# Four groups of TensorE transposes in a two-layer trunk handed to transposing transfers, with the attention's list of work rewritten

## The chip, the cores and the metric

The kernel runs on one core of one Trainium2 chip. The metric is the device time of one execution in microseconds (us). Before the change three runs gave 966.21 us in the median (965.93 to 966.33). One more execution was recorded by the hardware profiler; all rows below come from that one.

## The reference, cut to what matters

Two layers, 256 tokens, width 1024, fp32. Each layer is a feed-forward block, a mixer and another feed-forward block. The mixer of layer 0 is a gated recurrence, that of layer 1 is attention with a forget gate:

```python
# layer 0, mixer
gx = x @ w_in                                  # (256, 2 * 1344)
gate, rec = gx[..., :D_RNN], gx[..., D_RNN:]
rec = causal_depthwise_conv(rec, conv_w, conv_b)
rec = rg_lru(rec, w_a, b_a, w_x, b_x, lam)     # a scan over the tokens
return (jax.nn.gelu(gate) * rec) @ w_out
# layer 1, mixer, for each block of 128 tokens
logits = q @ k.T + c_q - c_k                   # 16 heads of 64, masked
p = jax.nn.softmax(logits, axis=-1)
o = p @ v
return o @ w_o
```

`jax.nn.gelu(gate)` comes out of its matrix product with tokens on the partitions, while the scan runs with channels on the partitions, so the gate has to be turned before the two are multiplied. The probabilities `p` likewise have to be turned before the product with `v`.

## The kernel before, in words

The 256 tokens are two halves, t=0 and t=1, of 128. Every large product is made of three fp32r products, high by high, high by low and low by high parts. A weight comes from HBM over SyncE's queue (SP) into one of five buffers `raw`. ScalarE (ACT) copies it to `whi` (L173) and VectorE (DVE) subtracts to get `wlo` (L177). TensorE (PE) then uses the pair for both halves, at L428, L429 and L432 in the feed-forward blocks and the q projection, and at L183 to L192 elsewhere.

PE's order is that of the program text. The work is a list of `items`, each with a preparation (load and split of a weight) and the products for one half. `slot` or `half` runs one of them. `defer(n, fn)` puts a small function n ticks behind, and `queue` with its costs lets out the recurrence's vector work in small portions. The other engines' order is made by a scheduler, which `high_priority` and `keep_in_program_order` steer. DMAs issued by SP stand in SP's order too.

**The recurrence.** `RG_ORDER` lists the items: `0g0` to `0g10` and `1g0` to `1g10` are the gate's products of the two halves, `r` those of the recurrent part, `gw` the small products of the two gates in the scan (L779, with a tanh at L793). A gate item that ends a column group copies its result from PSUM to `tok` (L686) and puts it on the list `plain`, whose Gelu comes later in `roots` (L840); only group 0 of half 0 gets its Gelu at once (L684). After the scan, `batch(g)` calls `gate_T` for both halves: four PE transposes each (L858) into PSUM, from which `product` (L867) multiplies into the scan's result. ACT (L868) and DVE (L873) split that for the output product.

**The attention.** `ATT_ORDER` is a string in which `0` and `1` are the next projection item of a half (first eight of q, then eight of the output), and `l0`, `n0`, `t0`, `v0` are steps of half 0: logits (L1146, sixteen matmuls for two head groups, then bias, row maximum and exponential on DVE and ACT at L1155 to L1162), norm (L1168, L1169), turn (four PE transposes at L1175 and a copy by ACT at L1177), and values (L1189). `l1` and so on are the same of half 1. Half 0 has four head groups of four heads, half 1 eight of two heads.

The q of half 1 is turned by a transfer already: `heads_T` scales it into `htok` (DVE, L996). `planes` (POOL, L212) sorts the fp32 words into two planes of 16-bit halves, `swap` (SP, L216) sends these through a transposing DMA, and `join` (POOL, L220) writes the words into `qT`, for which the logits `l1` wait.

Of the kernel before, what the change touches and what calls it, by code (L numbers as in the profile page):

```python
# [9 lines left out]
F32 = mybir.dt.float32  # L10
# [7 lines left out]
P = 128  # L18
# [25 lines left out]
def trunk_kernel(ctx: ExitStack, tc: tile.TileContext, A: dict, out: bass.AP):  # L44
# [13 lines left out]
    def nm(s):  # L58
        uid[0] += 1
        return f"{s}_{uid[0]}"  # L60
# [7 lines left out]
    def trbank():  # L68
        return psum.tile([P, 512], F32, tag="tr", name=nm("tr"), bufs=2)
# [11 lines left out]
    def defer(n, fn):  # L81
        pend.append([n, fn])
# [127 lines left out]
    def planes(dst, src):  # L210

        nc.gpsimd.tensor_copy(dst.rearrange("p (h f) -> p h f", h=2), src.bitcast(U16).rearrange("p (f h) -> p h f", h=2))  # L212

    def swap(turned, halves):

        tc.keep_in_program_order(nc.sync.dma_start(turned.rearrange("p (a b) -> p a b", b=P), halves, transpose=True))  # L216

    def join(dst, turned):

        nc.gpsimd.tensor_copy(dst, turned.rearrange("p (h f) -> p h f", h=2))  # L220
# [444 lines left out]
    def add_gate_unit(g, k0, kn):  # L665
        c0, nn = GCOLS[g]

        def prep():
            return split(load_raw(w_in(c0, nn, k0, kn), P, kn * nn), P, kn * nn)

        def work(t, u):
            if k0 == 0:
                gacc[(g, t)] = mmbank()
            ps = gacc[(g, t)][:, :nn]
            for j in range(kn):
                k = k0 + j
                mm3(ps, *main_x(t, k), u.hi[:, j * nn:(j + 1) * nn], u.lo[:, j * nn:(j + 1) * nn], k == 0, k == 7)
            if k0 + kn == 8:

                if t not in toks:  # L680
                    toks[t] = pools["r"].tile([P, DRNN], F32, name=f"tok{t}")
                tok = toks[t][:, c0:c0 + nn]
                if (g, t) == (0, 0):
                    nc.scalar.activation(tok, ps, AF.Gelu_apprx_tanh)  # L684
                else:
                    nc.scalar.activation(tok, ps, AF.Copy)  # L686
                    plain.append(tok)
        rg[f"g{sum(n[0] == 'g' and n[1] != 'w' for n in rg)}"] = len(items)
        items.append((prep, work))

    def tiles_of(p):
        return [2 * p, 2 * p + 1] if p < 5 else [10]
# [136 lines left out]
    def batch(g):  # L829

        pairs = [p for p in (2 * g, 2 * g + 1)]
        tps, ys = {}, {}

        def roots():
            for (a, b, w) in parts_of(g):
                v = tt[g][:w, a:b, :]
                nc.scalar.activation(v, v, AF.Sqrt)
            while plain:
                v = plain.pop(0)
                tc.keep_in_program_order(nc.scalar.activation(v, v, AF.Gelu_apprx_tanh))  # L840

        def u_of(p):
            w, m = pw(p), len(tiles_of(p))
            v = tt[g][:w, 2 * (p % 2):2 * (p % 2) + m, :]
            nc.vector.scalar_tensor_tensor(v, th[p][1][:w, :m, :], -1.0, v, ALU.mult, ALU.mult)
            nc.vector.tensor_tensor(v, v, xcs[p][:w, :m, :], ALU.mult)

        def scan(p, j):
            w = pw(p)
            v = tt[g][:w, 2 * (p % 2) + j, :]  # L850
            nc.vector.tensor_tensor_scan(v, th[p][0][:w, j, :], v, 0.0, ALU.mult, ALU.add)

        def gate_T(t):
            tok = toks[t][:, 4 * g * RT:]
            tp = tps[t] = trbank()
            for j in range(len(pairs) * 2 if g < 2 else 3):
                w = width(4 * g + j)
                nc.tensor.transpose(tp[:w, j * P:(j + 1) * P], tok[:, j * RT:j * RT + w], ident)  # L858

        def product(t):  # L860
            y = ys[t] = pools["r"].tile([RT, 4, P], F32, tag="y", name=nm("y"), bufs=2)
            if t == 0:
                yy[g] = [rw.tile([P, 1024], F32R, tag="gy", name=nm("y"), bufs=6).rearrange("p (t a b) -> p t a b", t=2, a=4)
                         for _ in range(2)]
            for (a, b, w) in parts_of(g):
                tp = tps[t][:w, a * P:b * P].rearrange("p (a b) -> p a b", a=b - a)
                nc.vector.tensor_tensor(y[:w, a:b, :], tp, tt[g][:w, a:b, t * P:(t + 1) * P], ALU.mult)  # L867
                nc.scalar.activation(yy[g][0][:w, t, a:b, :], y[:w, a:b, :], AF.Copy)  # L868

        def low(t):  # L870
            yh, yl = yy[g]
            for (a, b, w) in parts_of(g):
                nc.vector.tensor_tensor(yl[:w, t, a:b, :], ys[t][:w, a:b, :], yh[:w, t, a:b, :].bitcast(F32), ALU.subtract)  # L873

        key = ("y", g)
        q = [(0.0, key, roots)]
        for p in pairs:
            s = len(tiles_of(p)) / 2
            q.append((1.3 * s, key, lambda p=p: u_of(p)))
            q += [(0.72, key, lambda p=p, j=j: scan(p, j)) for j in range(len(tiles_of(p)))]  # L880
        q.append((0.0, key, lambda: (gate_T(0), gate_T(1))))
        for t in range(2):
# [26 lines left out]
    def load_gb(key, src):  # L909
        def f():  # L910
            gbox[key] = gain_bcast(src)
        return f
# [211 lines left out]
    def attention(t):  # L1124
# [41 lines left out]
        def norm(hg):  # L1166
            pe, sm = box["pe", hg], box["s", hg]
            nc.vector.reciprocal(sm, sm)  # L1168
            nc.vector.tensor_tensor(pe, pe, sm.unsqueeze(2).to_broadcast([P, per, nk * P]), ALU.mult)  # L1169

        def turn(hg):
            tp = trbank()
            pev = box["pe", hg].rearrange("p a b -> p (a b)")
            for j in range(4):
                nc.tensor.transpose(tp[:, j * P:(j + 1) * P], pev[:, j * P:(j + 1) * P], ident)  # L1175
            pT = box["pT", hg] = ap.tile([P, 4, P], F32, tag="pT", name=nm("pT"), bufs=4)
            nc.scalar.activation(pT.rearrange("p a b -> p (a b)"), tp, AF.Copy)  # L1177
# [25 lines left out]
    for n in range(2):  # L1203
# [2 lines left out]
    row_items(A["attn_w_o"][0], [P] * 8, lambda t, k: (att["oh"][t][:, k, :], att["ol"][t][:, k, :]),  # L1206
              lambda t, accs: enter(t, [main_dest(GI[("ffn2", 1)], t)], accs, gbox["mix1"], False, wait=4),
              rows0=1, late=True)
    ahead(n_q[0] + 2, load_gb("mix1", A["mix_post_g"][1]))
    n_att = len(items)  # L1210


    ffn_items(lambda: pools["f"], A["ffn2_w_gate"][1], A["ffn2_w_up"][1], A["ffn2_w_down"][1], A["ffn2_post_g"][1],
              lambda t: None, last=True)

    ATT_ORDER = ("0 0 0 0 0 0 0 l0 0 1 n0 l0 1 1 t0 n0 1 l0 v0 1 t0 n0 l0 1 v0 n0 1 t0 l1 1 v0 t0 n1 l1 0 v0 "
                 "n1 l1 t1 0 n1 l1 t1 0 n1 l1 v1 v1 t1 0 n1 l1 t1 0 n1 l1 v1 v1 t1 0 n1 l1 t1 0 n1 v1 v1 0 t1 1 "
                 "t1 v1 1 v1 1 1 1 1 1 1")

# [182 lines left out]
    steps = [attention(0), attention(1)]  # L1402
    nxt = [n_ffn3, n_ffn3]
    for c in ATT_ORDER.split():
        if c[0] in "lntv":
            with tc.high_priority():
                steps[int(c[1])][c[0]].pop(0)()
        else:
            half(int(c), nxt[int(c)])
            nxt[int(c)] += 1  # L1410
# [40 lines left out]
```

## Time and profile before

| | |
|---|---|
| median of three runs | 966.21 us |
| profiled execution | 966.79 us, of which 965.1 us are the span |
| PE busy | 957.0 us, 99% of the span |
| DVE, ACT, POOL busy | 639.8, 528.2, 209.1 us |
| PE in the chain that ended last | 95% |
| stage of the recurrence, gate products to turned gates | about 196 to 284 us |
| stage of the attention, half 0 and the q of half 1 | about 720 to 745 us |

A row of the timeline begins with its start and its length in microseconds, then engine, line, operation, what is written and what is read. A bracket at the end gives how long the engine sat idle before it and who released it. Matmuls overlap in the pipeline, so the pace of PE is read from starts, not from lengths.

### The profile page before, as it was taken

How to read it: one execution, taken by the hardware profiler on the slowest of the kernel's cores; microseconds unless marked ns; L12 is line 12 of the kernel's file. 1: busy time of each engine (PE TensorE's matmuls, PEld its weight loads, DVE VectorE, ACT ScalarE, POOL GpSimd, SP SyncE). 2: the span in 40 equal slices, each digit the busy share in tenths (PEclk: the TensorE clock that was granted, in tenths of full speed). 3: DMA queues.
4: the chain of work that ended last, by engine and by line, in shares of the span. 5: the costliest groups of instructions: out<-in, count | busy, mean ns of one | idle time of the engine just before them, and what ended most of it. 6: DMA issues, size and time to landing. Idle time of an engine off the chain costs nothing.

```text
span 965.1 us, 12873 instructions
## 1 busy us (share of the span) xinstructions
PE 957.0 (99%) x4583; PEld 792.3 (82%) x4583; DVE 639.8 (66%) x845; ACT 528.2 (55%) x751; POOL 209.1 (22%) x215
## 2 busy tenths in 40 slices
PE   9999999999999999999999999999999999999997
PEld 6888888898888888888898888888887788888886
DVE  6658764668998666664686566665488876666642
ACT  7446543568886555443565445444366855444431
POOL 2712330100001323230003623224122012232200
PEclk9999999999999999999999999999999999999999
DMA  8788996565337787786558979779763467777731
GB/s 284 227 247 235 267 275 196 156 197 158 121 107 235 204 234 216 202 239 200 136 175 284 248 223 264 225 184 283 237 246 108 133 199 236 207 217 239 221 110 44
DMA packets 146822, 198.27 MB, mean 205 GB/s; under 512 B 65054, under 2 KB 83846, under 8 KB 146630
## 3 DMA queue, kind: packets, MB, share of 16 engines
q1 hardware_dynamic: 144070, 190.53, 66.5%
q0 software_dynamic: 2080, 6.38, 2.3%
q8 instruction: 36, 0.59, 0.3%
q10 hardware_dynamic: 608, 0.53, 0.2%
q14 instruction: 28, 0.23, 0.1%
HBM read 182.19 MB, written 3.16 MB: 192 GB/s over the span
## 4 chain that ended last, share of the span: by engine, by line
PE 95%; DVE 2%; ACT 1%; issue 1%; POOL 0%; DMA 0%; POOLq 0%; DVEq 0%; ACTq 0%
PE mm L428 16%; PE mm L429 16%; PE mm L432 16%; PE mm L183 13%; PE mm L185 13%; PE mm L184 13%; PE gt L779 2%; PE mm L1286 1%; PE mm L190 1%; PE mm L191 1%; PE mm L192 1%; PE gt L226 1%; ACT pe L1162 1%; DVE wlo L177 0%; PE tr L127 0%
## 5 line engine op out<-in xcount | busy, mean ns | idle before, releaser
L177 DVE TENSOR_TENSOR wlo<-raw,whi 128x1024 fp32r<-128x1024 f32 (+5 forms) x329 | 416.5, 1272 | 228.7 <-ACT whi L173 227.7
L173 ACT ACTIVATE whi<-raw 128x1024 fp32r<-128x1024 f32 (+5 forms) x329 | 341.7, 1045 | 305.6 <-PE mm L432 133.5
L428 PE MATMUL mm<-whi,xhi 128*128 128x512 f32 x656 | 256.6, 391 | 0.0
L429 PE MATMUL mm<-wlo,xhi 128*128 128x512 f32 x656 | 255.5, 389 | 0.0
L432 PE MATMUL mm<-whi,xlo 128*128 128x512 f32 x656 | 202.2, 389 | 0.0
L432 PEld LDWEIGHTS mm<-whi,xlo 128*128 128x128 f32 x656 | 123.1, 188 | 26.0 <-DVE xlo L240 0.2
L428 PEld LDWEIGHTS mm<-whi,xhi 128*128 128x128 f32 x656 | 123.2, 188 | 25.8 <-issue 0.7
L429 PEld LDWEIGHTS mm<-wlo,xhi 128*128 128x128 f32 x656 | 123.2, 188 | 25.3 <-DVE wlo L177 0.3
L183 PE MATMUL mm<-whi,hhi 128*128 128x512 f32 x352 | 137.3, 390 | 0.0
L185 PE MATMUL mm<-whi,hlo 128*128 128x512 f32 x352 | 137.0, 389 | 0.0
L184 PE MATMUL mm<-wlo,hhi 128*128 128x512 f32 x352 | 137.0, 389 | 0.0
L540 POOL COPY pl<-prod 128x1024 uint16<-128x1024 uint16 (+1 forms) x48 | 68.4, 1424 | 169.0 <-DMA prod<-pl 168.9
L527 POOL COPY pl<-prod 128x1024 uint16<-128x1024 uint16 (+1 forms) x48 | 65.4, 1362 | 160.4 <-DVE prod L524 91.9
L185 PEld LDWEIGHTS mm<-whi,hlo 128*128 128x128 f32 x352 | 66.1, 188 | 13.8
L184 PEld LDWEIGHTS mm<-wlo,hhi 128*128 128x128 f32 x352 | 66.1, 188 | 13.7
L183 PEld LDWEIGHTS mm<-whi,hhi 128*128 128x128 f32 x352 | 66.1, 188 | 13.7 <-DVE prod L524 0.2
L198 POOL TENSOR_SCALAR nv<-ss 128x1 f32<-128x1 f32 x22 | 9.7, 439 | 284.2 <-ACT junk L205 284.2
L524 DVE SCALAR_TENSOR_TENSOR prod<-mm,rstd,sil 128x512 f32<-128x512 f32 (+1 forms) x48 | 33.8, 703 | 30.7 <-PE mm L432 24.9
L515 ACT ACTIVATE sil<-mm,rstd 128x512 f32<-128x512 f32 (+1 forms) x48 | 31.1, 651 | 33.1 <-PE mm L432 25.2
L546 DVE TENSOR_TENSOR hlo<-pl,hhi 128x512 fp32r<-128x512 f32 (+1 forms) x48 | 40.8, 849 | 5.9 <-ACT hhi L545 5.9
L183 PE MATMUL mm<-whi,xhi 128*128 128x512 f32 (+1 forms) x112 | 42.8, 382 | 0.0
L185 PE MATMUL mm<-whi,xlo 128*128 128x512 f32 (+1 forms) x112 | 42.5, 379 | 0.0
(219 smaller groups left out, 1050.2 us busy)
## 6 DMA issues: line engine op xcount, KB each, us to landing
raw<-in_ffn_w_down_dram SPq DMA_DIRECT2D x88, 512.0 KB
raw<-in_ffn_w_up_dram SPq DMA_DIRECT2D x80, 512.0 KB
raw<-in_ffn_w_gate_dram SPq DMA_DIRECT2D x78, 512.0 KB
raw<-in_rg_w_in_dram SPq DMA_DIRECT2D x10, 504.0 KB
raw<-in_rg_w_out_dram SPq DMA_DIRECT2D x10, 504.0 KB
raw<-in_ffn_w_gate_dram SPq DMA_DIRECT2D x19, 256.0 KB
raw<-in_ffn_w_up_dram SPq DMA_DIRECT2D x16, 256.0 KB
raw<-in_rg_w_in_dram SPq DMA_DIRECT2D x8, 512.0 KB
```

Of the source, the lines that this page charges most:

```text
L173: up = nc.scalar.activation(hi[:parts, c:c + m], rawv[:, c:c + m], AF.Copy)
L177: nc.vector.tensor_tensor(lo[:parts, c:c + m], rawv[:, c:c + m], hi[:parts, c:c + m].bitcast(F32), ALU.subtract)
L183: nc.tensor.matmul(ps, xh, wh, start=first, stop=False)
L184: nc.tensor.matmul(ps, xh, wl, start=False, stop=False)
L185: nc.tensor.matmul(ps, xl, wh, start=False, stop=last)
L428: nc.tensor.matmul(ps, get_x(t, k)[0], u.hi[:, c], start=k == 0, stop=False)
L429: nc.tensor.matmul(ps, get_x(t, k)[0], u.lo[:, c], start=False, stop=False)
L432: nc.tensor.matmul(ps, get_x(t, k)[1], u.hi[:, c], start=False, stop=k == nk - 1)
L524: nc.vector.scalar_tensor_tensor(pr[:, :nn], ps, rs[t][:, 0:1], s, ALU.mult, ALU.mult)
L527: nc.gpsimd.tensor_copy(halves.rearrange("p (h f) -> p h f", h=2), pr[:, :nn].bitcast(U16).rearrange("p (f h) -> p h f", h=2))
L540: nc.gpsimd.tensor_copy(halves.rearrange("p (f h) -> p h f", h=2), turned.rearrange("p (h a) b -> p h (a b)", h=2))
L546: keep(nc.vector.tensor_tensor(lv, x, hv.bitcast(F32), ALU.subtract))
```

## The change

In the recurrence, groups 0 and 1 of half 0 get their Gelu at once, and a new `gate_turn` turns them by transfer: a fill with zeros and a sorting copy on POOL, the transposing DMA on SP, a joining copy on POOL into the SBUF tile `tokT`. `gate_T` issues nothing for these, and `product` reads `tokT`. In the attention the first two head groups of half 0 are turned by `planes`, `swap` and `join`, in a tile that takes the buffer `gb`. The load of a gain into `gb`, which stood early on SP, becomes a step `g` of its own in the list, behind the values of the two groups.

```diff
@@ add_gate_unit
-                if (g, t) == (0, 0):
+                if t == 0 and g < 2:
                     nc.scalar.activation(tok, ps, AF.Gelu_apprx_tanh)
+                    defer(5 - 3 * g, lambda: gate_turn(g))
...
+    tokT = {}
+
+    def gate_turn(g):
+
+        halves = hpool.tile([P, 512], F32, tag="t1", name=nm("pl"), bufs=2).bitcast(U16)
+        hv = halves.rearrange("p (h j f) -> p h j f", h=2, j=4)
+        src = toks[0][:, 4 * g * RT:4 * (g + 1) * RT].bitcast(U16)
+        nc.gpsimd.memset(hv[:, :, :, RT:], 0)
+        nc.gpsimd.tensor_copy(hv[:, :, :, :RT], src.rearrange("p (j f h) -> p h j f", h=2, f=RT))
+        turned = pools["r"].tile([P, 512], F32, tag="turned", name=nm("turned"), bufs=1).bitcast(U16)
+        out = tokT[g] = pools["r"].tile([P, 4, P], F32, tag="tokT", name=nm("tokT"), bufs=2)
+        flat = out.rearrange("p a b -> p (a b)").bitcast(U16).rearrange("p (f h) -> p h f", h=2)
+        defer(1, lambda: swap(turned, halves))
+        defer(4, lambda: join(flat, turned))
...
         def gate_T(t):
+            if t == 0 and g < 2:
+                tps[t] = tokT[g].rearrange("p a b -> p (a b)")
+                return
...
+        def turn_by_transfer(hg):
+
+            if hg == 0:
+                box["two"] = hpool.tile([P, D], F32, tag="gb", name=nm("pT2"), bufs=1)
+            pT = box["two"][:, hg * 512:hg * 512 + 512]
+            turned = ap.tile([P, 512], F32, tag="pT", name=nm("turned"), bufs=4).bitcast(U16)
+            planes(pT.bitcast(U16), box["pe", hg].rearrange("p a b -> p (a b)"))
+            swap(turned, pT.bitcast(U16))
+            join(pT.bitcast(U16).rearrange("p (f h) -> p h f", h=2), turned)
+            box["pT", hg] = pT.rearrange("p (a b) -> p a b", a=4)
+
         def turn(hg):
+            if t == 0 and hg < 2:
+                turn_by_transfer(hg)
+                return
...
-    ahead(n_q[0] + 2, load_gb("mix1", A["mix_post_g"][1]))
...
-    ATT_ORDER = ("0 0 0 0 0 0 0 l0 0 1 n0 l0 1 1 t0 n0 1 l0 v0 1 t0 n0 l0 1 v0 n0 1 t0 l1 1 v0 t0 n1 l1 0 v0 "
+    ATT_ORDER = ("0 0 0 0 0 0 0 l0 0 1 n0 t0 l0 1 1 n0 t0 1 l0 1 n0 l0 1 n0 1 v0 v0 g t0 1 l1 v0 t0 n1 l1 0 v0 "
```

What this makes of the order on three engines. **POOL, attention.** Before, with the two turns of q for half 1 (`pl` and `htok` to `qT`) between two pairs of small operations of the norms:

```order
L198 TENSOR_SCALAR nv_6393<-ss_6390 128x1
L200 TENSOR_TENSOR rstd_6395<-nv_6393,mhalf 128x1
L212 COPY pl_6537<-htok_6535 128x1024
L220 COPY qT_6345<-htok_6535 128x2x512
L212 COPY pl_6655<-htok_6653 128x1024
L220 COPY qT_6345<-htok_6653 128x2x512
```

After:

```order
L212 COPY pT_1269_6491<-pe_6445 128x1024
L212 COPY pT_1269_6491<-pe_6457 128x1024
L220 COPY pT_1269_6491<-turned_6492 128x2x512
L212 COPY pl_6540<-htok_6538 128x1024
L220 COPY pT_1269_6491<-turned_6528 128x2x512
L220 COPY qT_6348<-htok_6538 128x2x512
L212 COPY pl_6630<-htok_6628 128x1024
L220 COPY qT_6348<-htok_6628 128x2x512
```

Three copies of the probabilities now stand ahead of the first sort of `htok`, and a fourth between it and its join.

**SP, attention.** Before, from the loads of the output weights to the second transfer of q:

```order
L164 DMA raw_6514<-in_attn_w_o_dram 128x1024
L343 DMA gb_6500<-in_mix_post_g_dram 128x1024
L164 DMA raw_6724<-in_attn_w_o_dram 128x1024
L164 DMA raw_6745<-in_attn_w_o_dram 128x1024
L164 DMA raw_6798<-in_attn_w_o_dram 128x1024
L216 DMA_TRANSPOSE htok_6535<-pl_6537 128x8x128
L164 DMA raw_6819<-in_attn_w_o_dram 128x1024
L161 DMA raw_6872<-in_ffn_w_gate_dram 128x2x512
L216 DMA_TRANSPOSE htok_6653<-pl_6655 128x8x128
```

After:

```order
L164 DMA raw_6722<-in_attn_w_o_dram 128x1024
L164 DMA raw_6743<-in_attn_w_o_dram 128x1024
L216 DMA_TRANSPOSE turned_6492<-pT_1269_6491 128x8x128
L216 DMA_TRANSPOSE turned_6528<-pT_1269_6491 128x8x128
L164 DMA raw_6796<-in_attn_w_o_dram 128x1024
L216 DMA_TRANSPOSE htok_6538<-pl_6540 128x8x128
L164 DMA raw_6817<-in_attn_w_o_dram 128x1024
L161 DMA raw_6870<-in_ffn_w_gate_dram 128x2x512
L343 DMA gb_6613<-in_mix_post_g_dram 128x1024
L216 DMA_TRANSPOSE htok_6628<-pl_6630 128x8x128
```

The two new transfers stand ahead of the first one of q, and the load of the gain has moved down, behind both.

**PE, attention.** Before, from the values of head group 1 to the first logits of half 1 (`mm` of L428 to L432 is the q projection, `gt` the logits):

```order
L1189 MATMUL mm_6576<-pT_6593,v_2938 64x128 x4
L428 MATMUL mm_6581<-whi_6297,xhi 128x512
L429 MATMUL mm_6581<-wlo_6298,xhi 128x512
L428 MATMUL mm_6581<-whi_6297,xhi 128x512
L429 MATMUL mm_6581<-wlo_6298,xhi 128x512
L432 MATMUL mm_6581<-whi_6297,xlo 128x512 x2
L1175 MATMUL tr_6617<-ident,pe_6553 128x128 x4
L1146 MATMUL gt_6624<-kT,qT_6345 128x256
L1146 MATMUL gt_6625<-kT,qT_6345 128x256
```

After (L1222, L1208 and L1165 are the same lines, moved down by the new text):

```order
L1222 MATMUL mm_6602<-pT_1269_6491,v_2941 64x128 x8
L1208 MATMUL tr_6615<-ident,pe_6556 128x128 x4
L428 MATMUL mm_6579<-whi_6306,xhi 128x512
L429 MATMUL mm_6579<-wlo_6307,xhi 128x512
L428 MATMUL mm_6579<-whi_6306,xhi 128x512
L429 MATMUL mm_6579<-wlo_6307,xhi 128x512
L432 MATMUL mm_6579<-whi_6306,xlo 128x512 x2
L1165 MATMUL gt_6634<-kT,qT_6348 128x256
L1165 MATMUL gt_6635<-kT,qT_6348 128x256
```

The values of groups 0 and 1 stand together, the turn of group 2 right behind them, and the last q item of half 1 stands ahead of the first logits of half 1 instead of behind them.

More of the change, by code (lines that the diff above doesn't have):

```diff
@@ L1404, in trunk_kernel @@
     for c in ATT_ORDER.split():
-        if c[0] in "lntv":
+        if c == "g":
+            load_gb("mix1", A["mix_post_g"][1])()
+        elif c[0] in "lntv":
             with tc.high_priority():
```

## The prediction, on record before the changed kernel ran

> **What bounds the kernel now.** The page comes first: busy times, the granted clock in 40 slices, the chain that ended last. Then PE's own list of waits.
>
> ```profile
> PE 957.0 (99%) x4583; PEld 792.3 (82%) x4583; DVE 639.8 (66%) x845; ACT 528.2 (55%) x751; POOL 209.1 (22%) x215
> PEclk9999999999999999999999999999999999999999
> PE 95%; DVE 2%; ACT 1%; issue 1%; POOL 0%; DMA 0%; POOLq 0%; DVEq 0%; ACTq 0%
> PE tr L127 <- PEq L1436: 0.8, 1, 0.8
> PE gt L779 <- issue: 0.5, 1, 0.5
> PE gt L1146 <- POOL qT L220: 0.3, 1, 0.3
> ```
>
> The reader is to see that PE is busy for 957.0 of 965.1 us, at a clock that never drops, and waits three times for 1.6 us in all. So work taken off PE is gained in full, a new wait of PE is lost in full, and behind the attention no slack gives it back. The third wait is in the stage that is rewritten.
>
> **What a group of four transposes costs PE.** The timeline of PE at the first turn in the attention:
>
> ```profile
> 728.36 0.60 PE L1175 MATMUL tr<-ident,pe 128*128 128x128 f32 x4
> 728.71 0.47 PE L428 MATMUL mm<-whi,xhi 128*128 128x512 f32 x1
> 729.02 0.39 PE L429 MATMUL mm<-wlo,xhi 128*128 128x512 f32 x1
> 729.25 0.39 PE L428 MATMUL mm<-whi,xhi 128*128 128x512 f32 x1
> ```
>
> From start to start the four take 0.35 us, and the product behind them 0.31 where the next takes 0.23: 0.43 us a group. The change takes away four groups, at most 4 x 0.43 = 1.72 us.
>
> **The recurrence.** Two groups go, one in each of these blocks of eight transposes; chain of waits, then ACT's timeline:
>
> ```profile
> 247.92 0.87 PE tr L858 x8
> 266.73 0.87 PE tr L858 x8
> 267.60 0.46 issue
> 257.27 1.57 ACT L793 ACTIVATE th<-gt,hb 126x256 f32<-126x256 f32 x4 [0.94 <-PE gt L779]
> 266.78 1.55 ACT L793 ACTIVATE th<-gt,hb 126x256 f32<-126x256 f32 x4
> ```
>
> The first half block is 0.87 / 2 = 0.44 us and is gained. The second is not: behind it PE stands still for 0.46 us, until the tanh at 266.78 has emptied a bank, and ACT works without a gap from 257.27, where it had waited for PE. ACT moves up by the first 0.44 only, so PE comes 0.44 earlier to a wait that grows by as much. (The Gelu that ACT no longer does in a batch stood before 257.27.) What could take the first gain back is POOL. Its new copies meet these rows of DVE, PE and ACT:
>
> ```profile
> 204.41 1.21 DVE L177 TENSOR_TENSOR wlo<-raw,whi 128x1008 fp32r<-128x1008 f32 x1 [2.14 <-ACT whi L173]
> 206.14 0.28 PE L192 MATMUL mm<-xhi,wlo 128*126 128x256 f32 x1
> 201.97 0.60 ACT L686 ACTIVATE tok<-mm 128x512 f32<-128x512 f32 x1 [0.86 <-PE mm L185]
> 215.82 1.05 ACT L173 ACTIVATE whi<-raw 128x1008 fp32r<-128x1008 f32 x1 [2.72 <-PE mm L191]
> ```
>
> Group 1's Gelu takes the place of the copy that ends at 202.57; the second sort (1.04, priced below) then runs to about 203.7, and the first join (1.37) starts between there and 204.0, beside the subtraction of 204.41. PE uses its result first at 206.14, a margin of 206.14 - 205.62 = 0.52. A join from 204.0 to 205.4 that shuts DVE out delays the subtraction by 0.97 and PE by 0.45. Bounds -0.44 and 0; I take -0.25, halfway. The two transfers hold SP for 1.24 each, ahead of a weight that ACT splits at 215.82, ten microseconds later: covered.
>
> **The attention: a port that two engines share.** The new copies run on POOL beside DVE's work. What that does is seen later in the kernel, on the timelines of DVE and POOL:
>
> ```profile
> 839.89 1.22 DVE L177 TENSOR_TENSOR wlo<-raw,whi 128x1024 fp32r<-128x1024 f32 x1
> 840.10 1.90 POOL L527 COPY pl<-prod 128x1024 uint16<-128x1024 uint16 x1 [6.21 <-ACT hhi L545]
> 841.02 1.52 DVE L546 TENSOR_TENSOR hlo<-pl,hhi 128x512 fp32r<-128x512 f32 x1
> ...
> L546 DVE TENSOR_TENSOR hlo<-pl,hhi 128x512 fp32r<-128x512 f32 (+1 forms) x48 | 40.8, 849 | 5.9 <-ACT hhi L545 5.9
> ```
>
> The sort issued at 840.10 takes 1.90, and the subtraction issued at 841.02 takes 1.52 where its group has a mean of 0.85. Both fit one reading: POOL's copy waits until L177 is done at 841.0, runs for about 1.0, and only then does DVE's next operation with two inputs in SBUF run. They take turns, in the order of issue, and a split holds the port for about 1.15 (839.89 to 841.02). The Trainium skill says the same ("SBUF — State Buffer", section "Who interferes with whom"): a GpSimd operation and a VectorE one with two SBUF inputs hold a shared port pair for a whole instruction each; these rows agree.
>
> Now the stage itself, POOL and SP, then DVE, then PE:
>
> ```profile
> 731.54 1.90 POOL L212 COPY pl<-htok 128x1024 uint16<-128x1024 uint16 x1 [14.43 <-DVE htok L996]
> 736.59 1.67 POOL L220 COPY qT<-htok 128x1024 uint16<-128x1024 uint16 x1 [3.15 <-DMA htok<-pl]
> 742.00 1.04 POOL L212 COPY pl<-htok 128x1024 uint16<-128x1024 uint16 x1 [3.75 <-DVE mx L1160]
> 746.17 1.37 POOL L220 COPY qT<-htok 128x1024 uint16<-128x1024 uint16 x1 [3.13 <-DMA htok<-pl]
> 733.47 1.24 SPq L216 DMA_TRANSPOSE htok<-pl  x1
> 726.76 0.69 DVE L1169 TENSOR_TENSOR pe<-pe,sm 128x512 f32<-128x512 f32 x1
> 729.52 1.23 DVE L177 TENSOR_TENSOR wlo<-raw,whi 128x1024 fp32r<-128x1024 f32 x1
> 731.33 1.22 DVE L177 TENSOR_TENSOR wlo<-raw,whi 128x1024 fp32r<-128x1024 f32 x1
> 734.29 1.22 DVE L177 TENSOR_TENSOR wlo<-raw,whi 128x1024 fp32r<-128x1024 f32 x1
> 736.36 0.69 DVE L1169 TENSOR_TENSOR pe<-pe,sm 128x512 f32<-128x512 f32 x1
> 742.63 0.96 DVE L1169 TENSOR_TENSOR pe<-pe,sm 128x512 f32<-128x512 f32 x1
> 746.50 1.00 DVE L1159 TENSOR_TENSOR mx<-mx,cq 128x2 f32<-128x2 f32 x1
> 737.45 0.60 PE L1175 MATMUL tr<-ident,pe 128*128 128x128 f32 x4
> 738.31 1.13 PE L1146 MATMUL gt<-kT,qT 64*128 64x256 f32 x8 [0.26 <-POOL qT L220]
> 739.38 0.50 PE L428 MATMUL mm<-whi,xhi 128*128 128x512 f32 x1
> 740.96 0.66 PE L1189 MATMUL mm<-pT,v 128*64 128x128 f32 x8
> ```
>
> Prices: an undisturbed sort 1.04, a join 1.37, the way from a sort's end to its join 3.14. The maximum's tiny addition at 746.50 takes 1.00 instead of 0.16 because the join at 746.17 has the port.
>
> PE without new waits: two groups less bring the turn of group 2 from 737.45 to 737.45 - 0.87 = 736.6. There is its input late? I go through the port in order, in the clock of before:
>
> - sort of group 0 behind its norm (726.76 + 0.69): 727.5 to 728.6; transfer, back at 731.7;
> - split 729.5 to 730.7; the sort of group 1, ready at 729.5, behind it: 730.7 to 731.7; back at 734.9;
> - the split of 731.33 behind that sort: 731.7 to 732.9;
> - join of group 0, ready since 731.7: 732.9 to 734.2;
> - sort of `htok`, fourth on POOL: 734.3 to 735.4 (before, it ended at 733.44); back at 738.5;
> - join of group 1: 735.4 to 736.8;
> - the split of 734.29: 736.8 to 738.0; then, after the reciprocal, the norm of group 2: 738.4 to 739.05 (before, 736.36 to 737.05).
>
> The port's users add up to 2 x 1.04 + 2 x 1.37 + 2 x 1.15 + 0.69 = 7.8 us between 730.7 and 738.5, so the order of the pieces hardly matters: the norm cannot end much before 738.5. Exponentials on ACT lie beside this. The values of group 1, which PE would reach some 0.6 before that turn, at 736.0, wait until 736.8; the turn of group 2 waits until 739.05. Behind it 0.43 and the moved q item, which took 740.96 - 739.38 = 1.58 at its old place and takes 1.46 behind transposes, bring the logits of half 1 to 740.9; their `qT` is joined by 739.05 + 1.37 = 740.4, so they add no wait. They take 1.07, and the values of group 2 start at 742.0 against 740.96: **+1.1 us**, with the 0.26 wait of before gone. Were nothing late, they would start at 736.6 + 0.43 + 1.46 + 1.07 = 739.6, -1.4.
>
> Next, the second sort of `htok` (742.00 before) now meets the norm of group 3. Before, it held that norm up by 0.96 - 0.69 = 0.27; now `htok` stands ahead of it on DVE, so it may wait for a whole sort: 0 to 1.04, I take 0.5. The load of the gain into `gb` moves behind the values; its first reader is at 764.24, in this row, some 25 us later, so it is hidden:
>
> ```profile
> 764.24 1.28 DVE L284 TENSOR_TENSOR t<-mm,gb 128x512 f32<-128x512 f32 x2
> ```
>
> ACT loses two copies and was not waited for. Sum: -0.25 + 1.1 + 0.5 = **+1.35 us**. The profiled execution goes from 966.79 to 968.14; it lay 0.58 above the median of the runs, so the time is 966.21 + 1.35 = **967.6 us**. Bounds of this case: -0.44 + 0.6 + 0 (norm at 738.5) = +0.2, and 0 + 1.1 + 2.2 = +3.3, where sort and join of the second `htok` each hold DVE's chain up by about 1.1 in turn.
>
> The Trainium skill has a rule against this edit, in "VectorE: DVE Perf Modes", section "The three transpose paths": 390 ns for 128x128 on TensorE and 1309 ns through the DMA's crossbar, TensorE preferred where PSUM will do. The rows have 0.35 for four fp32 blocks on PE and 3.14 for a group's transfer; so by the rule each turned group is later, and only cover decides, as in the sum.
>
> **Rivals.**
>
> 1. *The gain stands.* POOL's copies fit between DVE's operations, or the scheduler's order of the wide splits leaves PE fed: the turn of group 2 waits less than 0.9. For it: the sort at 742.00 ran in 1.04 beside DVE, since there DVE had work from PSUM. Against it: the two long POOL rows of 731.54 and 736.59 in this very stage. Attention -1.4 to 0, recurrence -0.25: 964.5 to 966.2, some 965.2.
> 2. *A slide to half 1, slower than the band.* Half 1's groups are a chain of logits, norm, turn with PE's output products between. If the second sort and join both cut into it, its turns come 1 to 3 us late and PE has no other work: +2.2 to +5, 968.4 to 971. It decides once the two `htok` copies delay the norm of group 3 or the first norm of half 1 by over 1.3 us together. For it: at 746.50 a join cost DVE 0.84. Against it: half 1 has several output products ahead.
> 3. *All gains come.* PE loses all four groups, the 0.26 wait and some of the 0.46: -2 to -2.3, 964.0. This needs the stall behind 266.73 to shrink though ACT sets its end.
>
> **How the numbers follow.** About 0.2% (1.93 us) is what a measurement of this kernel can tell from no change: faster is below 964.28, slower above 968.14. The forecast gets 0.55; its bounds, +0.2 to +3.3, put 0.35 of that within and 0.20 above. Rival 1 gets 0.25, all within; rival 2 gets 0.13, above; rival 3 gets 0.07, below. Faster 0.07, same 0.60, slower 0.33. The range takes rival 1 from 964.6 and the lower part of rival 2, to 969.6.
>
> **What would show it.** After the change PE's list of waits should name the turn of group 2 (L1208, released by DVE's norm) with 1.5 to 2.5 us and the values of group 1 (L1222, POOL's join) with about 1; new POOL copies of 1.9 beside splits; in the recurrence eight transposes less, and a wait at L779 of about 0.9. If the turn of group 2 waits less than 0.9 us, the port is not the price that I think, and rival 1 holds. If PE waits in half 1 instead, it is rival 2.

## The result, and the profile after

The changed kernel takes 968.93 us in the median of seven runs (968.11 to 969.93), the kernel before, with four runs more than above, 966.25 (965.93 to 966.67): +2.68 us, or 0.28% slower by the medians. The ratio on record, an estimate from all runs that need not equal the quotient of the medians, is 1.0026 with a 95% interval of 1.0016 to 1.0036. So it is slower. The profiled execution took 969.32 us with a span of 967.6.

First the page of the changed kernel, the two lines that answer to those of before, and PE's own list of waits (L1208, L1222, L795 and L1188 are the old L1175, L1189, L779 and L1169):

```profile
PE 955.8 (99%) x4567; PEld 791.1 (82%) x4567; DVE 643.5 (67%) x845; ACT 526.9 (54%) x748; POOL 223.0 (23%) x225
PEclk9999999999999999999999999999999999999999
...
PE tr L1208 <- DVE pe L1188: 2.5, 3, 1.3
...
PE gt L795 <- issue: 0.8, 1, 0.8
PE mm L1222 <- POOL pT L220: 0.4, 1, 0.4
PE mm L1222 <- ACT pT L1210: 0.3, 1, 0.3
```

PE has sixteen instructions less, and in place of one wait of 0.3 in the attention it has five, of 3.2 us together. The clock's row shows nothing: its slices of 24 us are too wide for what the windows below show. Where the time went is read from the distance between the same instruction in both traces. At the first long products the changed kernel's execution is already 0.46 us early (6.06 below against 6.52 before; that part was not changed). At 260 it is 0.90 early, at 656 1.04, and at 762, behind the attention, 2.27 late. So the recurrence gave about 0.45 and the attention of this execution cost 3.3.

PE's timeline at these places:

```profile
6.06 0.48 PE L1318 MATMUL mm<-whi,xlo 128*128 128x512 f32 x1
...
267.15 1.06 PE L795 MATMUL gt<-xc,gw 84*84 84x256 f32 x4 [0.84 <-issue]
...
735.17 0.66 PE L1222 MATMUL mm<-pT,v 128*64 128x128 f32 x8 [0.37 <-POOL pT L220]
737.17 0.63 PE L1208 MATMUL tr<-ident,pe 128*128 128x128 f32 x4 [1.34 <-DVE pe L1188]
737.56 0.48 PE L428 MATMUL mm<-whi,xhi 128*128 128x512 f32 x1
...
740.10 1.71 PE L1165 MATMUL gt<-kT,qT 64*128 64x256 f32 x8
741.74 0.66 PE L1222 MATMUL mm<-pT,v 128*64 128x128 f32 x8
742.81 0.63 PE L1208 MATMUL tr<-ident,pe 128*128 128x128 f32 x4 [0.41 <-DVE pe L1188]
...
747.26 0.63 PE L1208 MATMUL tr<-ident,pe 128*128 128x128 f32 x4 [0.78 <-DVE pe L1188]
```

The wait in the recurrence grew from 0.46 to 0.84, so of two groups of transposes one was gained. In the attention the values of group 1 wait for their join, then the turns of groups 2 and 3 and the first turn of half 1 wait for their norms. Who held up the norms stands on POOL and DVE:

```profile
728.54 2.04 POOL L212 COPY pT<-pe 128x1024 uint16<-128x1024 uint16 x1 [0.98 <-ACT whi L173]
730.79 2.09 POOL L220 COPY pT<-turned 128x1024 uint16<-128x1024 uint16 x1 [0.20 <-DMA turned<-pT]
732.79 1.04 POOL L212 COPY pl<-htok 128x1024 uint16<-128x1024 uint16 x1
733.78 1.34 POOL L220 COPY pT<-turned 128x1024 uint16<-128x1024 uint16 x1
...
741.08 1.04 POOL L212 COPY pl<-htok 128x1024 uint16<-128x1024 uint16 x1 [2.00 <-DVE htok L1015]
745.28 1.34 POOL L220 COPY qT<-htok 128x1024 uint16<-128x1024 uint16 x1 [3.16 <-DMA htok<-pl]
```

```profile
728.46 1.23 DVE L177 TENSOR_TENSOR wlo<-raw,whi 128x1024 fp32r<-128x1024 f32 x1
730.26 1.40 DVE L177 TENSOR_TENSOR wlo<-raw,whi 128x1024 fp32r<-128x1024 f32 x1
732.97 0.88 DVE L1179 TENSOR_TENSOR mx<-mx,cq 128x4 f32<-128x4 f32 x1
734.19 1.95 DVE L177 TENSOR_TENSOR wlo<-raw,whi 128x1024 fp32r<-128x1024 f32 x1
736.34 0.69 DVE L1188 TENSOR_TENSOR pe<-pe,sm 128x512 f32<-128x512 f32 x1
...
741.14 1.53 DVE L1188 TENSOR_TENSOR pe<-pe,sm 128x512 f32<-128x512 f32 x1
745.60 1.51 DVE L1188 TENSOR_TENSOR pe<-pe,sm 128x512 f32<-128x512 f32 x1
```

Read by turns: the sort of group 1 waits for the split of 728.46 and takes 2.04; the first join waits for the next split and takes 2.09; a tiny addition (732.97) waits for the sort of `htok`, the third split (734.19, 1.95) for the second join. Later the norm of group 3 takes 1.53 instead of 0.69 because the sort of the second `htok` was issued 0.06 earlier, and the norm of 745.60 takes 1.51 because of the join of 745.28.

Last, the windows of PE's clock in this stretch (busy times of the engines, then the granted clock as third number from the end):

```profile
738.20:739.20 1.00, 1.00 (x4) 0.75 (x3) 0.39 (x1) 1.00 (x5) 0.88 (x1) 0.50 0.93 328
739.20:740.20 1.00, 1.00 (x5) 0.35 (x3) 0.00 (x0) 0.00 (x0) 0.00 (x0) 0.50 1.03 365
740.20:741.20 1.00, 1.00 (x6) 0.82 (x8) 0.90 (x3) 0.00 (x0) 0.12 (x1) 0.50 0.92 367
741.20:742.20 1.00, 1.00 (x14) 0.62 (x10) 1.00 (x1) 0.00 (x0) 0.92 (x1) 0.94 0.22 80
```

Soon after the wait of 1.34 the clock is halved, for some 3.4 us (windows of 0.1 us put it from 737.9 to 741.3). The q item from 737.56 to 740.10 takes 2.54 instead of 1.46 and the logits 1.64 instead of 1.07, together 1.6 more. Not all of that is lost by the cut: the wait for group 3's norm is 0.41 here, but 0.98 in the run of the attention alone below, whose clock holds. From the turn of the second q to the last values, the changed kernel takes 0.96 longer than that run. So about 1.0 of the 3.3 lost in this execution is the clock.

### The profile page after: what moved, and what is told of

The parts are those of the page before. It is cut to its first block, busy times and chain, and to the rows that moved or that the text cites. A ratio compares the mean times of both kernels' runs of the same rounds, so it can differ in the third digit from the quotient of the medians.

```text
span 967.6 us, 12857 instructions
## 1 busy us (share of the span) xinstructions
PE 955.8 (99%) x4567; PEld 791.1 (82%) x4567; DVE 643.5 (67%) x845; ACT 526.9 (54%) x748; POOL 223.0 (23%) x225
## 4 chain that ended last, share of the span: by engine, by line
PE 94%; DVE 3%; ACT 1%; issue 1%; DMA 0%; POOLq 0%; POOL 0%; ACTq 0%; DVEq 0%
PE mm L428 16%; PE mm L429 16%; PE mm L432 16%; PE mm L183 13%; PE mm L185 13%; PE mm L184 13%; PE gt L795 2%; PE mm L1318 1%; PE mm L190 1%; PE mm L191 1%; PE mm L192 1%; ACT pe L1181 1%; DVE wlo L177 1%; PE gt L226 1%; DVE pe L1174 1%
## 5 line engine op out<-in xcount | busy, mean ns | idle before, releaser
L428 PE MATMUL mm<-whi,xhi 128*128 128x512 f32 x656 | 256.6, 391 | 0.0
L432 PE MATMUL mm<-whi,xlo 128*128 128x512 f32 x656 | 202.6, 390 | 0.0
L432 PEld LDWEIGHTS mm<-whi,xlo 128*128 128x128 f32 x656 | 123.4, 188 | 26.1 <-DVE xlo L240 0.3
L428 PEld LDWEIGHTS mm<-whi,xhi 128*128 128x128 f32 x656 | 123.3, 188 | 25.5
L540 POOL COPY pl<-prod 128x1024 uint16<-128x1024 uint16 (+1 forms) x48 | 70.8, 1474 | 170.5 <-DMA prod<-pl 170.5
L527 POOL COPY pl<-prod 128x1024 uint16<-128x1024 uint16 (+1 forms) x48 | 67.1, 1399 | 153.1 <-DVE prod L524 88.1
```

The lines of the kernel that those rows point to most:

```text
L428: nc.tensor.matmul(ps, get_x(t, k)[0], u.hi[:, c], start=k == 0, stop=False)
L432: nc.tensor.matmul(ps, get_x(t, k)[1], u.hi[:, c], start=False, stop=k == nk - 1)
L527: nc.gpsimd.tensor_copy(halves.rearrange("p (h f) -> p h f", h=2), pr[:, :nn].bitcast(U16).rearrange("p (f h) -> p h f", h=2))
L540: nc.gpsimd.tensor_copy(halves.rearrange("p (f h) -> p h f", h=2), turned.rearrange("p (h a) b -> p h (a b)", h=2))
```

## The experiments

The theory: the copies on POOL and DVE's two-input operations exclude each other, and norms that come late through this make PE wait. The rivals: the rewritten order is at fault; the transferred blocks themselves come late; each transferred group costs by itself. "Way" is the time on PE from the turn of the second q of half 0 (726.54 before) to the values of group 2, and from there on to the last values of half 1, each in the profiled execution (before: 14.42 and 27.52; changed kernel: 16.27 and 29.02).

| run | median us | before us | ratio, 95% interval | way |
|---|---|---|---|---|
| gates alone | 966.08 | 966.39 | 0.9999, 0.9990 to 1.0008 | as before |
| attention alone | 968.77 | 966.39 | 1.0026, 1.0017 to 1.0035 | 14.77, 29.56 |
| list alone | 966.49 | 966.39 | 1.0003, 0.9994 to 1.0012 | 14.24, 27.84 |
| transfers that nobody uses | 967.96 | 966.39 | 1.0016, 1.0007 to 1.0025 | 15.45, 28.76 |
| one group | 967.39 | 966.43 | 1.0007, 0.9998 to 1.0016 | 14.89, 28.15 |
| one join on ACT | 968.03 | 966.43 | 1.0016, 1.0007 to 1.0025 | 14.27, 28.90 |
| q item first | 967.50 | 966.45 | 1.0011, 1.0002 to 1.0020 | 14.39, 28.67 |
| splits later, with transfers | 976.87 | 966.45 | 1.0105, 1.0089 to 1.0120 | 13.37, not comparable |
| splits later, without | 978.09 | 966.45 | 1.0120, 1.0106 to 1.0133 | 13.68, not comparable |
| gates, group 2's Gelu later | 965.42 | 966.43 | 0.9990, 0.9981 to 0.9999 | as before |
| gates, one more Gelu at once | 965.21 | 966.40 | 0.9984, 0.9975 to 0.9993 | as before |

**Gates alone.** The recurrence's part of the diff on the kernel before.

> Only the recurrence's part: the gates of half 0, groups 0 and 1, are turned by transfer; the attention and its list are as before. Theory of the port (the loss is made in the attention, where POOL's copies shut out DVE): 0.45 us less than before, 965.8, with eight PE transposes fewer and the one wait for a bank at L795 longer by about 0.4 (0.8 to 0.9). Rival, that the recurrence's copies cost something too: no less than before, 966.2 or more.

Measured 966.08, 0.31 below before, which the interval does not tell from nothing: three of its eleven executions took 967.6 to 967.9, and why is open. The trace does tell: the same products are 0.43 earlier behind the recurrence than ahead of it, and the wait at L795 is 0.8. No other wait is new, so the trace shows no loss through POOL.

**Attention alone.** The attention's part of the diff, the gates as before.

> Only the attention's part, the gates as before. Theory of the port: 3.1 us more than before in the median, 969.4; executions in which TensorE's clock is cut after the wait for group 2's norm lie about 1.1 above the others. Rival, that part of the loss is made in the recurrence: below 968.5.

Measured 968.77, +2.38 where 3.1 was expected. This profiled execution has no clock cut, so its waits are the loss itself (L1189 is the turn, L1203 the values):

```profile
736.06 0.66 PE L1203 MATMUL mm<-pT,v 128*64 128x128 f32 x8 [0.43 <-POOL pT L220]
738.06 0.63 PE L1189 MATMUL tr<-ident,pe 128*128 128x128 f32 x4 [1.34 <-DVE pe L1169]
742.72 0.63 PE L1189 MATMUL tr<-ident,pe 128*128 128x128 f32 x4 [0.98 <-DVE pe L1169]
747.12 0.63 PE L1189 MATMUL tr<-ident,pe 128*128 128x128 f32 x4 [0.74 <-DVE pe L1169]
763.65 0.66 PE L1203 MATMUL mm<-pT,v 128*64 128x128 f32 x8 [0.31 <-ACT pT L1191]
```

The first two, 1.77, use up what the removed transposes and the old wait gave, and 0.35 more (14.77 against 14.42). The other three, 2.03, are the 2.04 by which the second part of the way is longer. So most of the loss is made behind the values of group 2. The last of the three is no norm: the list alone, next, has a wait of 0.43 at the same place. Two of the eleven executions took 969.60 and 969.87, some 1.0 above the median, as was expected of executions with a cut; whether they have one isn't shown.

**List alone.**

```diff
-"0 0 0 0 0 0 0 l0 0 1 n0 l0 1 1 t0 n0 1 l0 v0 1 t0 n0 l0 1 v0 n0 1 t0 l1 1 v0 t0 n1 ..."
+"0 0 0 0 0 0 0 l0 0 1 n0 l0 1 1 t0 n0 1 l0 1 t0 n0 l0 1 n0 1 v0 v0 g t0 1 l1 v0 t0 n1 ..."
```

> The rewritten list without a transfer: all groups are turned by PE, groups 0 and 1 at their old places, but their values stand together behind three q items, the last q item of half 1 stands ahead of the first logits of half 1, and the gain is loaded at its new place. Theory of the port: 0.2 to 0.4 less than before (the wait of 0.26 goes), 965.9 to 966.1. Rival, the order is at fault (values too late, the turn of group 2 too early): 968 or more, with PE waiting at the turns of groups 2 and 3 for their norms.

Measured 966.49, +0.10, and no wait for a norm. The small gain that was expected did not come. The wait for `qT` is 0.49, not gone, and a late copy by ACT makes a new one, by which the second part of the way is 0.32 longer:

```profile
761.20 0.66 PE L1189 MATMUL mm<-pT,v 128*64 128x128 f32 x8 [0.43 <-ACT pT L1177]
```

But the order is not what costs 2.4 us.

**Transfers that nobody uses.** The list alone, with `c0` (sort, transfer, join as in the change, into tiles that are not read) behind the norms of groups 0 and 1.

```diff
-"... 0 1 n0 l0 1 1 t0 n0 1 l0 1 t0 ..."
+"... 0 1 n0 c0 l0 1 1 t0 n0 c0 1 l0 1 t0 ..."
```

> The same list and the same PE transposes, and beside them the four POOL copies and two transfers of groups 0 and 1 run as in the changed kernel, into a tile that nobody reads. Nobody waits for a transferred block, so only what the copies do to other engines is left. Theory of the port: PE waits at the turn of group 2 for its norm, by 0.5 to 1.3, and at later turns as in the changed kernel; 2.0 to 3.3 more than before, 968.3 to 969.5. Rival, that the transferred blocks come late to the values: as the list alone, 965.9 to 966.2.

Measured 967.96: +1.57 against before and +1.47 against the list alone, a little under the range. PE has all its transposes, waits for no transferred block, and yet

```profile
737.99 0.63 PE L1186 MATMUL tr<-ident,pe 128*128 128x128 f32 x4 [1.27 <-DVE pe L1169]
```

So 1.5 us of loss come from what the transfers' work does to others. That it is POOL's four copies rather than the two DMAs is shown by the rows of DVE and by the held-back splits below; this run doesn't part them. The attention alone is 0.8 worse still, though PE has eight transposes less.

**One group.** Group 0 by transfer, group 1 turned by PE at its old place.

```diff
-            if t == 0 and hg < 2:
+            if t == 0 and hg < 1:
                 turn_by_transfer(hg)
...
-"... 1 1 n0 t0 1 l0 1 n0 l0 1 ..."
+"... 1 1 n0 1 l0 1 t0 n0 l0 1 ..."
```

> The attention's part with only head group 0 turned by transfer; group 1 is turned by PE again at its old place, the rest of the list as in the changed kernel, the gates as before. One sort and one join less on the port. Theory of the port: the norm of group 2 comes about 2 us earlier than with two groups, PE waits for it 0.3 at most, and the time is within 0.4 of before, 966.0 to 966.8. Rival, each transferred group costs by itself (its block comes late, or POOL handles one after the other): half the loss of two groups, about 967.6.

Measured 967.39, +0.96: the theory, as I had sized it, missed, and half the loss of two groups came nearer. Its waits (turn of group 2, logits of half 1):

```profile
736.90 0.63 PE L1189 MATMUL tr<-ident,pe 128*128 128x128 f32 x4 [0.70 <-DVE pe L1169]
739.76 1.13 PE L1146 MATMUL gt<-kT,qT 64*128 64x256 f32 x8 [0.86 <-POOL qT L220]
```

The port need not be full. One copy in the chain from row maximum over exponential to norm is enough, here the sort of `htok`, issued at 733.07:

```profile
733.25 0.88 DVE L1160 TENSOR_TENSOR mx<-mx,cq 128x4 f32<-128x4 f32 x1
```

The addition takes 0.88 instead of 0.16 in the list alone, and the norm of group 2 ends 10.81 behind the turn of the second q instead of 10.06. PE, with a group of transposes less to do, meets it. The second wait is in part a queue: the sort of `htok`, behind the join of group 0, ends 1.3 later than before. Another 1.1 is the way of its transfer, 4.26 instead of 3.15, and that isn't the group's doing: the list alone has 4.52.

**One join on ACT.**

```diff
-            join(pT.bitcast(U16).rearrange("p (f h) -> p h f", h=2), turned)
+            dst = pT.bitcast(U16).rearrange("p (f h) -> p h f", h=2)
+            if hg == 0:
+                nc.scalar.activation(dst, turned.rearrange("p (h f) -> p h f", h=2), AF.Copy)
+            else:
+                join(dst, turned)
```

> The attention's part with both groups by transfer, but the join of group 0 is made by ACT instead of POOL: 1.34 us less on the port that POOL and DVE share, and the sort of htok no longer stands behind that join. ACT is idle about there. Theory of the port: the norm of group 2 comes about 1.3 earlier, and the time falls from 968.8 to 967.0 to 967.8. Rival, that the turn of group 2 waits for something else than the port: 968.5 to 969.

Measured 968.03: 0.7 better than the attention alone, just short of the range.

```profile
736.73 0.66 PE L1207 MATMUL mm<-pT,v 128*64 128x128 f32 x8 [1.06 <-POOL pT L220]
737.60 0.63 PE L1193 MATMUL tr<-ident,pe 128*128 128x128 f32 x4 [0.21 <-DVE pe L1169]
742.19 0.63 PE L1193 MATMUL tr<-ident,pe 128*128 128x128 f32 x4 [0.93 <-DVE pe L1169]
```

The wait for the norm of group 2 fell from 1.34 to 0.21, but only in part because the norm is earlier: counted from the turn of the second q it ends at 11.11 instead of 11.62, 0.5 earlier and not 1.3, and PE comes later to it, since the values of group 1 now wait 1.06 for their join. That join starts when it did, but beside the third split (734.28), and then itself holds up an addition of DVE (735.42, 1.22 instead of 0.15):

```profile
734.74 1.93 POOL L220 COPY pT<-turned 128x1024 uint16<-128x1024 uint16 x1 [1.32 <-DMA turned<-pT]
```

So the port set the wait, and what was taken off it was more than half used up by new collisions. The wait for group 3's norm stayed.

**Splits later, with and without transfers.** The other side of the port: DVE's three splits of output weights are held back.

```diff
+        if n_q[0] <= i <= n_q[0] + 3 and hold[0] and not must:
+            return
...
-            if settled[0] or pin:
+            if settled[0] or pin or n_q[0] <= state["p"] <= n_q[0] + 2:
                 tc.keep_in_program_order(up)
...
         if c == "g":
+            hold[0] = False
```

> The attention's part with both groups by transfer and every copy on POOL as in the changed kernel, the gates as before; but the three splits of output weights that DVE made among those copies (729.5, 731.3 and 734.3 in the profile of before) are held back until the token g and come behind the second htok. Theory of the port: with 3.4 us of two-input work gone from the stretch, the copies of POOL start when they are ready, the norm of group 2 comes over 1.5 us earlier than with the splits, PE does not wait for it, and most of the loss goes: 966.2 to 967.4. Rival, the transfers' own way (sort, DMA, join one behind another) is what comes late: as the attention's part, 968.4 to 969.

> Control for the held-back splits: the rewritten list with all groups turned by PE, and the same three splits held back. Theory of the port: nothing to gain where POOL has only the two htok turns, 966.0 to 966.8, as the list alone. Rival, that holding the splits back is a gain or a loss by itself: off by more than 0.5.

Both totals missed by ten microseconds, and in the second run the rival came true: holding the splits back costs by itself. The output weights then come late to everything behind, PE waits for them (rows of the run with transfers), it waits for a norm in half 1 (1.60 with transfers, 2.71 without), and the clock is cut twice in each run:

```profile
PE mm L183 <- ACT whi L173: 3.2, 2, 2.3
PE mm L184 <- DVE wlo L177: 2.7, 4, 1.0
```

What can be compared is the way to the values of group 2, which lies ahead of that. Without the splits beside them the same copies run undisturbed, and the turn of group 2 waits less, though it still waits:

```profile
729.37 1.04 POOL L212 COPY pT<-pe 128x1024 uint16<-128x1024 uint16 x1 [0.98 <-DVE pe L1172]
731.57 1.34 POOL L220 COPY pT<-turned 128x1024 uint16<-128x1024 uint16 x1 [1.16 <-DMA turned<-pT]
```

```profile
736.66 0.63 PE L1192 MATMUL tr<-ident,pe 128*128 128x128 f32 x4 [0.59 <-DVE pe L1172]
```

2.04 became 1.04 and 2.09 became 1.34, and that turn starts 1.40 earlier, counted from the turn of the second q, where over 1.5 was expected. With the splits the transfers make this way longer than the list alone (14.77 against 14.24), without them shorter (13.37 against 13.68). Put otherwise, holding the splits back gains 0.56 without transfers and 1.40 with them; the 0.84 between is what copies and splits cost each other. So the transfers' own way is not what is late; the exclusion is.

**q item first.** The turn of group 2 stands behind the last q item.

```diff
-"... v0 v0 g t0 1 l1 v0 t0 n1 ..."
+"... v0 v0 g 1 t0 l1 v0 t0 n1 ..."
```

> The attention's part with the turn of group 2 behind the last q item of half 1 instead of ahead of it, so PE has 1.46 us of work while that group's norm is late. Theory, that PE's saved transposes became waiting because no work covers the late norm: the wait at that turn goes, but then the logits of half 1 wait about 1.0 for their qT, which comes no earlier; later norms meet the second sort about 1.3 earlier. 968.0 to 968.8 against 968.8 of the attention's part. Rival, that the place of the turn alone makes the loss: 967 or less.

Measured 967.50, +1.05 against before, 1.3 better than the attention alone, where up to 0.8 was expected; the rival's 967 was not reached either, so part of the loss hangs on the place of the turn. The profiled execution took 969.06, 1.6 above the median; it is 1.3 late already at the turn of the second q, ahead of what was changed, so that its way can be compared. As expected the wait moves to `qT`:

```profile
741.18 1.13 PE L1146 MATMUL gt<-kT,qT 64*128 64x256 f32 x8 [0.90 <-POOL qT L220]
743.47 0.63 PE L1189 MATMUL tr<-ident,pe 128*128 128x128 f32 x4 [0.57 <-DVE pe L1169]
```

The wait for group 3's norm is 0.57 instead of 0.98, and the one at the first turn of half 1 is gone.

**Gates, group 2's Gelu later; then one more Gelu at once.** From the loss to a gain: the 0.84 at L795.

```diff
-                    plain.append(tok)
+                    plain.append((g, tok))
...
-            while plain:
-                v = plain.pop(0)
+            mine = [n for n in plain if n[0] <= g]
+            plain[:] = [n for n in plain if n[0] > g]
+            for _, v in mine:
```

> The gates by transfer as in the run of the gates alone, and in addition the Gelu of column group 2 is kept out of the second batch of ACT's late Gelus (it comes with the third batch). Theory, that ACT's chain sets the end of the wait at L795: ACT reaches that tanh 0.4 earlier, the wait falls from 0.84 to about 0.45, and the time is 0.4 below that of the gates alone, about 965.7. Rival, that the wait is set by something else: as the gates alone, 966.1.

```diff
+                elif g == 1:
+                    nc.scalar.activation(tok, ps, AF.Gelu_apprx_tanh)
...
+            if not mine:
+                tc.keep_in_program_order(nc.scalar.activation(warm, mhalf, AF.Gelu_apprx_tanh))
```

> The gates by transfer with group 2's Gelu held back, as in that run, and in addition the Gelu of group 1, half 1, taken at once where the result is copied out of PSUM; the second batch then has a Gelu of one column only, in its old place. Theory, that ACT's chain ends the wait at L795: ACT comes another 0.5 earlier, the wait falls from 0.48 to nearly nothing, and the time is 965.0, 0.4 below the run with group 2 held back alone and 1.4 below before. Rival, that something else ends that wait by then (PE's own sequence, the copies into the scan): 965.4, as that run.

Measured 965.42 and 965.21. PE at the place of the wait, in the first and in the second:

```profile
267.16 1.06 PE L795 MATMUL gt<-xc,gw 84*84 84x256 f32 x4 [0.48 <-issue]
```

```profile
266.83 1.06 PE L797 MATMUL gt<-xc,gw 84*84 84x256 f32 x4
```

0.84, 0.48, nothing: the wait was ACT's chain. The second kernel is 1.2 us faster than before, where the changed one is 2.7 slower. Its last 0.2 lies within the spread of the two (965.14 to 966.22 and 964.87 to 965.42).

**Pauses.** Does waiting halve the clock? Twelve pauses of PE in the blocks behind the recurrence of the kernel before, each of one to three round trips:

```diff
+    def pause(k):
+        v = ident
+        for _ in range(k):
+            tp = trbank()
+            nc.tensor.transpose(tp[:, :P], v, ident)
+            v = spool.tile([P, P], F32, tag="pause", name=nm("pause"), bufs=1)
+            with tc.high_priority():
+                nc.vector.tensor_copy(v, tp[:, :P])
+        nc.tensor.transpose(trbank()[:, :P], v, ident)
+    for i in range(12):
+        defer(30 + 20 * i, lambda i=i: pause(1 + i % 3))
```

> The kernel before with twelve pauses of PE added in the feed-forward blocks and the key and value products behind the recurrence: a transpose, a copy of its result by DVE, a transpose of the copy, once, twice or three times in a row. What is computed from the inputs is unchanged. If waits of PE are what halves the granted clock, the cut should follow pauses of over 1.5 us in all and none of the short ones (under 0.9 us), and matmuls behind it should take about twice as long for 3 us. If the cut of the changed kernel came from elsewhere, no pause is followed by one, or short and long ones alike.

One execution, 998.25 us. By the sum of its waits, seven pauses came to 0.38 to 0.93 and five to 1.95, 2.13, 2.76, 2.85 and 3.24. Behind none of the seven is the clock below 0.98 in any window of 1 us; behind three of the five (1.95, 2.76, 3.24) it is 0.50 for 3.4 us. All three had three round trips; the 2.85 had two, the 2.13 three. One with a cut and one without, PE's rows and the windows behind them:

```profile
375.24 0.33 PE L1403 MATMUL tr<-ident,pause 128*128 128x128 f32 x1 [1.92 <-DVE pause L1402]
...
491.59 0.33 PE L1399 MATMUL tr<-ident,pause 128*128 128x128 f32 x1 [1.83 <-DVE pause L1402]
492.38 0.33 PE L1399 MATMUL tr<-ident,pause 128*128 128x128 f32 x1 [0.46 <-DVE pause L1402]
```

```profile
376.00:377.00 1.00, 1.00 (x6) 0.81 (x5) 0.00 (x0) 0.00 (x0) 0.00 (x0) 1.00 0.77 105
...
494.00:495.00 1.00, 1.00 (x4) 0.80 (x3) 1.00 (x2) 0.00 (x0) 0.00 (x0) 0.50 0.00 0
```

So waits of some 2 us in all, close together, can halve the clock and need not (the changed kernel had a cut with 0.37 and 1.34, the attention alone none with 0.43 and 1.34); what decides between them is open.

## Why the prediction held, step by step, and where it was off

The time, 968.93, lies in the stated range, and slower is the side that the forecast of +1.35 leaned to. But +2.68 is over the bound of 0.2%, a case that had a chance of 0.33, and twice the forecast. That the sum came so near is in part luck, since errors cancel: the chain to the values of group 2 was priced 0.75 too dear, the second `htok` 1.2 too cheap, and the clock not at all. By its steps:

1. **The recurrence: right.** One group gained, the other swallowed: the wait was to grow from 0.46 to about 0.9 and is 0.84. The loss to POOL, for which I halved the gain to -0.25, did not come: -0.44 in the trace. The first join ran at 205.27, behind the split that I feared for, and held up the next one (205.32, 2.31 instead of 1.21) without making PE wait.
2. **The port and its order of turns: right in mechanism.** Every piece that I queued appears in that order. The norm of group 2 was to end 2.0 later than before; measured from the turn of the second q, it ends 1.05 later (11.56 against 10.51). My seven pieces, from the end of the first split to the end of the norm, took 8.35 (730.7 to 739.05); measured it is 7.34 (729.69 to 737.03). I added full recorded lengths, but most hand over up to 0.1 before their recorded end (the sort of 732.79 starts while the join of 730.79 is recorded until 732.88), and the 0.4 that I left ahead of the norm is 0.2 (736.14 to 736.34). So the limit that I drew, that the norm cannot end much before 738.5, does not hold either: in the clock of before it ends at 738.1. The turn waits 1.34 where I had said 1.5 to 2.5, the values of group 1 wait 0.37 where I had said about 1, and the values of group 2 come 0.35 later in the attention alone, not 1.1.
3. **The second `htok`: the mis-sized term.** I took 0.5 for its sort, and left its join out of the sum; only the upper bound, 2.2, had both. Measured in the attention alone, the sort costs 0.98 at the norm of group 3 and the join 0.74 at the first norm of half 1: 1.72, towards the upper end. (The other 0.31 of the second part of the way is the late copy by ACT, which the list alone has too; it was no term of the sum.) I had named both collisions in the bounds and then took a low value, because one row before showed 0.27. The new order puts `htok` directly ahead of the norm on DVE, and then the whole copy counts.
4. **The clock: missed.** I took the granted clock as fixed. In the profiled execution a cut costs about 1.0, against the attention alone without one. Of the seven runs three took 969.32 to 969.93 at a mean clock of 0.996 to 0.997, four 968.11 to 968.93 at 0.998 to 0.999. That the three are those with the cut is shown for the profiled one alone.
5. **The rivals.** That the gain stands fell: every run with both groups by transfer waits for norms, also those in which the splits or a join are moved, only less. That all gains come fell with it: the wait at L795 grew. The slide into half 1 is half of what happened. Its two collisions came and cost 1.72, more than the 1.3 at which I had said that it decides, and 968.93 lies in its band as well as in that of the forecast; but the turns of half 1 behind these two are not late any more.

Two parts measured alone add up to -0.31 + 2.38 = +2.07, the change to +2.68; its four executions at the higher clock have a median of 968.61, which is +2.36. So half of the remaining 0.6 would be that more of its executions have the cut; the rest stays open.

## What to carry to other kernels

An engine that is on no critical path is not free if it shares a port with one that is: add the lengths of everything that needs the port in the stretch, and look at what each new copy stands directly ahead of. Work that is taken off the bounding engine ahead of a chain that is only just in time turns into waiting there; here it paid where the next wait was also shortened (the Gelus), and not where more was put beside the chain.

## What the runs showed of the hardware that was not expected

- TensorE's granted clock went to 0.50 after two waits of 0.37 and 1.34 us within 2.4 us, with matmuls between them, and after three of the five longer pauses. Each of these cuts lasted 3.4 us, and so did three of the four in the runs with the splits held back; the fourth lasted 6.8. The attention alone had 0.43 and 1.34 at the same place and no cut. The Trainium skill ("TensorE: Matmul & The Clock Gate", Part 1: The HAM clock gate) has the clock halved after an idle window of about 3.4 us; here no single wait of PE in any run was longer than 2.71, and none ahead of the cuts behind the pauses longer than 1.85, so the length of a single gap is not the whole rule.
- The way of a transposing transfer is not fixed: from the end of the sort of the first `htok` to its join it took 3.15 us before, 3.91 in the changed kernel, 4.26 with one group and 4.52 with the list alone, where nothing else was transposed beside it. SP issued it within 0.03 of the sort's end in each of them (733.86 after 733.83 in the changed kernel); what makes the difference is open.
